# Other recorded distances in stage 1 of a hybrid decoder step: small products, the sample's chunk and the bonus sums

## The chip, the cores and the metric

The kernel runs on one core of a Trainium2 chip. The metric is the device time in microseconds (us) of one execution. Each profile is of one execution, and its rows are of that execution alone. Engines are named as the profile does: PE is TensorE, PEld its weight loads, DVE VectorE, ACT ScalarE, POOL GpSimd and SP SyncE, which issues most DMAs.

## The reference

The reference computes one layer of a decoder for two groups of requests: one prompt of 1024 tokens, and 8 samples of 8 tokens each, which are laid side by side as 1088 columns. Features lie on partitions.

```
h  = adaLN(RMSNorm(x), c)
P  = h @ w_in                       # RWKV columns | pooling columns | gate columns
A  = RWKV-7(P)                      # token shift, decay, delta-rule state per head, group norm, bonus, gate
B  = pooling over windows 2/4/8/16, minus the token, a linear map per group, a scale
x += gate * ((sigmoid(gA) * (A @ w_br_rwkv) + sigmoid(gB) * (B @ w_br_pool)) @ w_out)
h  = adaLN(RMSNorm(x), c)
x += gate * (relu(h @ w_ff1)**2 @ w_ff2)
y  = RMSNorm(x)
```

The state of RWKV-7 follows, per head of 64 values, `S = S*w + (S @ -kk) (kk*a) + v k` and `y = S r`. The bonus is `sum(r*k*r_k) * v` over a head.

## The kernel before, in words

**Stage 1** (`phase1`) computes P, the RWKV and pooling branches and `B @ w_br_pool`; **stage 2** (`phase2`) the rest. The large products are *streamed*: a weight of 128 x 512 is loaded, ACT copies it to `whi` in a 32-bit format that TensorE takes in one pass, and `wlo` = weight - `whi` is made by POOL for odd weights and by DVE for even ones (`weights`). Each column block of 364 or 362 is multiplied three times (hi x hi, hi x lo, lo x hi), so a weight of 512 columns is 36 streamed products (`mm<-hx,whi` and `mm<-hx,wlo` in the rows). At most two weights are held at a time.

Between the streamed products stand the small ones of the heads. The 8 heads go as 4 *pairs* f = 0 to 3, each through these steps:

- `front(f)`: decay and gate logits (`sw` products, tanh), the cumulative decay on DVE, the norm of kk (`bones` products, a square root on ACT, reciprocals on DVE at line 302), the operands `bk` (lines 561 on DVE and 562 on POOL), `q` (568) and the bonus sums (three products with `bones`, then a multiply into `bv` at 577).
- `sample(f - 1)`: the chunk of the samples of the pair before, which has its own state.
- `scores(f)`: three `unit`s (8 chunks of 64 tokens, the samples' chunk, 8 more chunks): products of keys, `ab`/`ak` masks, transposes.
- `inverse`, `level`, `affine`: the inverse of a triangular matrix per chunk, by DVE and then by small products (L726, L737), and what follows from it.
- `chain(f)`: the 16 steps of the state; each is a product with the state S, then a DVE operation that makes the next S (line 828).
- `post(f)`: group norm (`bones` products, reciprocals, lines 926 to 935), bonus and gate.

Beside them `pools` does the pooling groups (`px` and `plw` products, z at lines 457 to 468).

**The order.** Each step is a generator that yields a distance; `Pace` keeps a clock of its own, which every product moves on by an estimate from its shape (a streamed one by n/2.4 + 14 ns). A step whose distance has passed is taken first, and else the next three streamed products are recorded. So the distances alone set where a small product stands in TensorE's order, which is kept as recorded:

```
self.pace.t += n / 2.4 + 14 if rhs.dtype == F32R else max(n / 0.6 * min(mode) / 128, 30) + 3
```

The other engines' queues are ordered by a scheduler, from the recording. Small products write the PSUM tiles `w`, of which there are two, or `wc`, also two; a third waits until the first is read. Five `wt` rows hold the vectors of a pair.

Of the kernel before, what the change touches and what calls it, by code (L numbers as in the profile page):

```python
# [18 lines left out]
P = 128  # L19
# [98 lines left out]
class K:  # L118
    def __init__(self, tc, io):
        self.tc, self.nc, self.io = tc, tc.nc, io  # L120
        self.n = 0
        self.nw = 0
        self.pace = Pace()
        self.mode = None
        self.done = set()

# [27 lines left out]

    def weights(self, src, eng=None):

        nc = self.nc
        n = self.nw
        self.nw += 1
        raw = self.wp.tile([P, 512], F32, tag="wraw", bufs=WB[0], name=self.nm("wraw"))  # L160
        nc.sync.dma_start(raw, src)
        hi = self.wp.tile([P, 512], F32R, tag="whi", bufs=WB[1], name=self.nm("whi"))
        lo = self.wp.tile([P, 512], F32R, tag="wlo", bufs=WB[1], name=self.nm("wlo"))
        nc.scalar.activation(hi, raw, AF.Copy)  # L164
        (eng or (nc.gpsimd if n % 2 else nc.vector)).tensor_tensor(lo, raw, hi.bitcast(F32), op=ALU.subtract)  # L165
        return [(hi[:, q * 128:(q + 1) * 128], lo[:, q * 128:(q + 1) * 128]) for q in range(4)]
# [313 lines left out]
    def pools(self):  # L480

        nc = self.nc
        self.pl = {}
        for g in range(4):
            plw = self.pxp.tile([P, P], F32, tag="plw", bufs=1, name=self.nm("plw"))
            nc.sync.dma_start(plw, self.io["pool_w"][:, g * 128:(g + 1) * 128])
            yield lambda: ("pool", g) in self.done
            yield 5000 + 1300 * g
            z, zs, hi, lo = self.pl[g]
            for c0, n in CH:  # L490
                m = min(n, NPR - c0)
                ps = self.ps("w")
                self.mm(ps[:, :m], plw, z[:, c0:c0 + m], start=True, stop=True)
                if m < n:
                    self.mm(ps[:, m:n], plw, zs, start=True, stop=True)
                sc = self.par("pool_scale", g)
                nc.scalar.activation(hi[:, c0:c0 + n], ps[:, :n], AF.Copy, scale=sc)
                nc.vector.scalar_tensor_tensor(lo[:, c0:c0 + n], ps[:, :n], sc, hi[:, c0:c0 + n].bitcast(F32), op0=ALU.mult, op1=ALU.subtract)
                yield 600
            nc.sync.dma_start(self.d_op[0][g], hi.bitcast(F32))  # L500
            nc.sync.dma_start(self.d_op[1][g], lo.bitcast(F32))
            self.done.add(("op", g))


    def front(self, f):
# [9 lines left out]
        t1, tha = self.wt(), self.wt()  # L515
        yield 9000 if f == 0 else 4500
        for c0, n in CH:
            ps = self.ps("w")
            self.mm(ps[:, :n], w2a2[0:64, :], wa[0:64, c0:c0 + n], start=True, stop=True)
            nc.scalar.activation(t1[:, c0:c0 + n], ps[:, :n], AF.Tanh, bias=self.hp[:, f:f + 1], scale=0.5)  # L520
            ps = self.ps("w")
            self.mm(ps[:, :n], w2a2[64:128, :], wa[64:128, c0:c0 + n], start=True, stop=True)
            nc.scalar.activation(tha[:, c0:c0 + n], ps[:, :n], AF.Tanh, bias=self.hp[:, 4 + f:5 + f], scale=0.5)
            yield 0
        nc.gpsimd.tensor_scalar(t1, t1, 1.0, None, op0=ALU.add)
# [21 lines left out]
        nc.scalar.activation(sq, kk, AF.Square)  # L547
        yield 9000
        for c0, n in CH:
            ps = self.ps("w")  # L550
            self.mm(ps[:, :n], self.kc("bones"), sq[:, c0:c0 + n], start=True, stop=True)
            self.rinv(ps, n, sq[:, c0:c0 + n], 1.0, 1)
            yield 0
        nc.vector.tensor_tensor(kk, kk, sq, op=ALU.mult)
# [10 lines left out]
        nc.sync.dma_start(r, self.d_x[f])  # L565

        q = self.wt()
# [3 lines left out]
        nc.sync.dma_start(v, self.d_x[8 + f])  # L571
        bv = self.wt()
        yield 12000
        for c0, n in CH:
            ps = self.ps("w")
            self.mm(ps[:, :n], self.kc("bones"), q[:, c0:c0 + n], start=True, stop=True)
            nc.vector.tensor_tensor(bv[:, c0:c0 + n], ps[:, :n], v[:, c0:c0 + n], op=ALU.mult)
            yield 0
        nc.sync.dma_start(self.d_bv[f], bv)
        self.cur = dict(bk=bk, end=end, v=v, kk=kk, r=r, ev=ev, es=es, z=self.z, qs={})  # L580

    def scores(self, f, d):

        d["ad"], d["ao"] = self.iv(), self.sm.tile([P, 16, 32], F32, tag="ao", bufs=1, name=self.nm("ao"))
        self.nc.gpsimd.memset(d["ad"][:, NC:32, :], 0.0)
        yield from self.unit(f, d, 0)
        yield from self.unit(f, d, 2)
        yield from self.unit(f, d, 1)

    def unit(self, f, d, u):  # L590
# [17 lines left out]
        else:  # L608
            nc.vector.scalar_tensor_tensor(cut8(ra[:, 0, 1, :]), cut8(kk[:, NPR:NT]), -1.0, es[:, :, 0:8], op0=ALU.mult, op1=ALU.mult)
            nc.gpsimd.tensor_tensor(cut8(ra[:, 0, 0, :]), cut8(r[:, NPR:NT]), es[:, :, 1:9], op=ALU.mult)  # L610
            strict, incl = self.kc("strict8"), self.kc("incl8")
        yield 2500 if prompt else 1200
        for a in range(0, C, 4):
# [8 lines left out]
            for h, (hs, ps) in enumerate(zip(HB, pss)):  # L622
# [4 lines left out]
                for b in range(2):  # L627
# [6 lines left out]
                    else:  # L634
                        nc.vector.tensor_tensor(ad[rq, 16, :], src[:, 0, :], strict[rq, 32 * b:32 * b + 32], op=ALU.mult)
            yield 2500
        bh = bk[:, cs, :, :].rearrange("p c s j -> p c (s j)")
# [39 lines left out]
    def inverse(self, d):  # L677
# [33 lines left out]
        d["zd"], d["xd"], d["n16"] = zd, xd, cut32(n16)  # L711
        yield 2500

    def level(self, d):
# [11 lines left out]
        nc.vector.tensor_tensor(nd, cut32(ps), self.kc("i32").unsqueeze(1).to_broadcast([P, 16, 32]), op=ALU.add)  # L726
        yield 1500
        ps, px = self.ps("w"), self.ps("w")
# [9 lines left out]
        for os in HB:  # L738
            for b in (1, 0):
                rq = slice(os.start + 32 * b, os.start + 32 * b + 32)  # L740
                nc.scalar.activation(z[rq, :16, 32 * b:32 * b + 32], cut32(ps)[rq], AF.Copy)
        yield 1500
        ps = self.ps("w")
# [6 lines left out]
        for os in HB:  # L750
            hi = slice(os.start + 32, os.start + 64)
            nc.scalar.activation(pt[hi], cut32(ps)[hi], AF.Copy)
        yield 1500
        ps = self.ps("w")
# [5 lines left out]
        for os in HB:  # L760
            lo = slice(os.start, os.start + 32)
            nc.scalar.activation(z[lo, :16, 32:64], cut32(ps)[lo], AF.Copy)
        yield 1200

# [39 lines left out]
    def chain(self, f, d):  # L804
# [4 lines left out]
        for u in range(2):  # L809
# [9 lines left out]
            for i in range(8):  # L819
# [11 lines left out]
                S = S1  # L831
                yield LS
            us = slice(u * 512, (u + 1) * 512)
# [11 lines left out]
    def sample(self, f, d):  # L845
# [7 lines left out]
        qm = self.kc("qm")  # L853
        um = iv()
        yield 3000
        px = self.ps("w")
        for h, hs in enumerate(HB):
            os = HB[1 - h]
            if h:
                yield 1500  # L860
            ps = self.ps("w")
            self.mm(ps[os, :], ra[hs, 0, 1, :], s0[hs, :], start=True, stop=True, tile_position=(hs.start, os.start))
            nc.vector.tensor_tensor(qv(um[os]), qv(ps[os, :]), qm[os].unsqueeze(2).to_broadcast([64, 8, 64]), op=ALU.mult)
            self.mm(px[os, 0:64], ak[hs, 0, :], uv[hs, 0, h, :], start=True, stop=True, tile_position=(hs.start, os.start))
        x = sm.tile([P, 64], F32, tag="xs", bufs=1, name=self.nm("x"))
        nc.vector.tensor_reduce(x, um.rearrange("p (q v) -> p v q", v=64), axis=AX.X, op=ALU.add)
        nc.vector.tensor_tensor(x, x, px[:, 0:64], op=ALU.add)
        yield 2500
        for os in HB:
            self.mm(px[os, 64:128], z[os, 16, :], x[os, :], start=True, stop=True)  # L870
        for h, os in enumerate((HB[1], HB[0])):
            nc.scalar.activation(uv[os, 0, h, :], px[os, 64:128], AF.Copy)
        yield 1200
        py = self.ps("w")
# [6 lines left out]
        else:  # L881
            y = sm.tile([P, 64], F32, tag="ys", bufs=1, name=self.nm("y"))
            nc.scalar.activation(y, py[:, :64], AF.Copy)
            nc.sync.dma_start(self.d_y[f][:, NPR:NT], y)
        pn = self.ps("w")
        for h, hs in enumerate(HB):
# [3 lines left out]
            yield 1200  # L890
            self.mm(pn[hs, :], ab[:, 0, h, 64:128], um, start=True, stop=True)
        nc.gpsimd.tensor_tensor(qv(s0), qv(s0), end[:, 16:24].unsqueeze(2).to_broadcast([P, 8, 64]), op=ALU.mult)
# [3 lines left out]
    def post(self, f):  # L896
# [25 lines left out]
        def piece(c0, n):  # L922
# [4 lines left out]
            nc.scalar.activation(sq[:, s], y[:, s], AF.Square)  # L927
            yield 3000
            ps = self.ps("w")
# [39 lines left out]
    def heads(self):  # L969

        for f in range(4):
            yield from self.front(f)
            d = self.cur
            if f > 0:
                yield from self.sample(f - 1, self.ds[f - 1])
            yield from self.scores(f, d)
# [149 lines left out]
    def or_rows(self):  # L1126

        yield lambda: "op" in self.done
        for j in range(3):
            for i in range(2):  # L1130
                t = self.orr[i][j] = self.row(self.hx, "hx", 16, F32R)
# [245 lines left out]
NC = 17  # L1377
LS = 900
WB = (2, 2)
# [72 lines left out]
```

## Time and profile before

| | us |
|---|---|
| median of 3 runs | 1920.29 |
| lowest and highest | 1919.14, 1922.01 |
| the profiled execution | 1926.83 |
| its span, from the first to the last instruction | 1925.1 |
| PE busy in the span | 1765.1 (92%) |
| DVE, ACT, POOL busy | 884.6, 564.1, 374.4 |
| mean granted TensorE clock | 0.946 |

In the page's slices a digit is a tenth of a slice of 48 us. The streamed products begin at 52 us, and stage 2 follows on the reload of rows near 922 to 940 us. In a row of groups the shape of one operation is followed by its count, the busy time, the mean ns of one, and the idle time of the engine just before it with what ended that. In a row of the timeline the brackets hold the idle time ahead of it and what ended that.

### The profile page before, as it was taken

The numbers are of one execution on the slowest core, as the hardware profiler recorded it, in microseconds if no ns is written. First come the engines' busy times: TensorE is split into PE (matmuls) and PEld (weight loads), VectorE is DVE, ScalarE is ACT, GpSimd is POOL, SyncE is SP. The second block draws the span as 40 slices with busy tenths as digits, with TensorE's granted clock in tenths as the row PEclk, the third lists the DMA queues.
The fourth block names the chain that finished last, engine by engine and source line by source line (L and its number), as shares of the span: only waits on it lengthen the run. The fifth ranks groups of instructions, "written<-read, shape, count | busy, mean of one in ns | idle before, by whom it ended". The sixth has DMA issues, their size and how long they took to land. (4 is left out here: it accounts for less than half of the span.)

```text
span 1925.1 us, 32541 instructions
## 1 busy us (share of the span) xinstructions
PE 1765.1 (92%) x13721; PEld 1621.9 (84%) x13721; DVE 884.6 (46%) x1484; ACT 564.1 (29%) x1085; POOL 374.4 (19%) x406
## 2 busy tenths in 40 slices
PE   3889897988799889899899889999999999999997
PEld 1779776876587669789788879999999999999997
DVE  5476445665456455533342664242424242424335
ACT  4424241443134414431122443131313131312132
POOL 1551114101210130001231441111111111111110
PEclk8889788989899899899899989999999999999998
DMA  8232313121322141226772211111111111111112
GB/s 303 73 109 90 108 48 121 56 99 58 124 79 72 55 144 52 71 90 226 265 274 99 77 61 52 48 45 44 45 45 44 44 45 44 44 44 45 44 50 93
DMA packets 76450, 169.97 MB, mean 88 GB/s; under 512 B 15152, under 2 KB 21808, under 8 KB 76304
## 3 DMA queue, kind: packets, MB, share of 16 engines
q1 hardware_dynamic: 70688, 151.68, 22.8%
q10 hardware_dynamic: 5472, 15.70, 2.4%
q8 instruction: 108, 1.77, 0.4%
q0 software_dynamic: 144, 0.51, 0.1%
q14 instruction: 38, 0.31, 0.1%
HBM read 133.47 MB, written 34.39 MB: 87 GB/s over the span
## 5 line engine op out<-in xcount | busy, mean ns | idle before, releaser
L146 PE MATMUL mm<-hx,whi 128*128 128x362 f32 (+1 forms) x2560 | 686.0, 350 | 6.9 <-DMA hx<-d_orl 3.5
L146 PEld LDWEIGHTS mm<-hx,whi 128*128 128x128 f32 x2560 | 461.4, 196 | 47.4 <-issue 21.2
L146 PE MATMUL mm<-hx,wlo 128*128 128x362 f32 (+1 forms) x1280 | 429.6, 336 | 5.2 <-DVE wlo L165 5.0
L165 POOL TENSOR_TENSOR wlo<-wraw,whi 128x512 fp32r<-128x512 f32 x120 | 166.3, 1386 | 1070.9 <-ACT whi L164 1047.2
L146 PE MATMUL mm<-ma,whi 128*128 128x364 f32 (+1 forms) x1280 | 317.6, 329 | 0.0
L164 ACT ACTIVATE whi<-wraw 128x512 fp32r<-128x512 f32 x240 | 151.2, 631 | 559.8 <-PE w L146 395.0
L146 PEld LDWEIGHTS mm<-hx,wlo 128*128 128x128 f32 x1280 | 251.7, 197 | 6.1 <-DVE wlo L165 5.6
L146 PEld LDWEIGHTS mm<-ma,whi 128*128 128x128 f32 x1280 | 225.9, 188 | 5.1 <-issue 4.3
L146 PE MATMUL mm<-ma,wlo 128*128 128x364 f32 (+1 forms) x640 | 210.1, 328 | 0.0
L1330 DVE SCALAR_TENSOR_TENSOR hx<-mm,aq,hx 128x364 f32<-128x364 f32 (+4 forms) x136 | 75.0, 588 | 215.1 <-PE mm L146 214.9
L146 PE MATMUL w<-mb,whi 128*128 128x362 f32 x640 | 164.3, 338 | 6.0 <-DVE mb L1225 2.1
L165 DVE TENSOR_TENSOR wlo<-wraw,whi 128x512 fp32r<-128x512 f32 x120 | 93.6, 780 | 154.0 <-ACT whi L164 153.9
L146 PEld LDWEIGHTS w<-mb,whi 128*128 128x128 f32 x640 | 117.5, 196 | 8.3 <-DVE mb L1225 2.6
L146 PEld LDWEIGHTS mm<-ma,wlo 128*128 128x128 f32 x640 | 120.5, 188 | 0.0
L1243 DVE TENSOR_TENSOR ft<-ft 128x362 f32<-128x362 f32 (+1 forms) x96 | 51.7, 562 | 137.1 <-ACT ft L1242 136.8
L146 PE MATMUL w<-mb,wlo 128*128 128x362 f32 x320 | 107.9, 337 | 7.1 <-DVE wlo L165 5.8
L146 PE MATMUL w<-hx,whi 128*128 128x362 f32 x416 | 104.1, 332 | 0.0
L146 PEld LDWEIGHTS w<-hx,whi 128*128 128x128 f32 x416 | 74.0, 192 | 0.9 <-issue 0.9
L1335 POOL TENSOR_TENSOR hx<-hx,rs 128x64 f32<-128x64 f32 x72 | 36.7, 510 | 187.1 <-DVE rs L1333 187.0
L146 PEld LDWEIGHTS w<-mb,wlo 128*128 128x128 f32 x320 | 62.8, 196 | 8.6 <-DVE wlo L165 7.0
L146 PE MATMUL w<-wt,kct 128*128 128x362 f32 (+1 forms) x96 | 46.0, 586 | 26.1 <-DVE wt L568 10.6
L1242 ACT ACTIVATE ft<-mm 128x364 f32<-128x364 f32 x64 | 29.3, 474 | 134.5 <-PE mm L146 134.4
(295 smaller groups left out, 2374.3 us busy)
## 6 DMA issues: line engine op xcount, KB each, us to landing
wraw<-in_w_ff SPq DMA_DIRECT2D x132, 256.0 KB, 2.6
wraw<-in_w_in SPq DMA_DIRECT2D x68, 256.0 KB, 2.8
t<-in_w_ada_mlp SPq DMA_DIRECT2D x24, 512.0 KB, 5.4
wt<-d_x SPq DMA_DIRECT2D x20, 544.0 KB, 3.9
d_th<-px SPq DMA_DIRECT2D x16, 544.0 KB, 3.3
aw<-in_w_ada_mix SPq DMA_DIRECT2D x16, 512.0 KB, 10.0
wraw<-in_w_out SPq DMA_DIRECT2D x32, 256.0 KB, 2.6
d_x<-d SPq DMA_DIRECT2D x14, 512.0 KB, 2.6
```

What stands on the lines that cost most here:

```text
L146: return self.nc.tensor.matmul(out, lhsT, rhs, **kw)
L164: nc.scalar.activation(hi, raw, AF.Copy)
L165: (eng or (nc.gpsimd if n % 2 else nc.vector)).tensor_tensor(lo, raw, hi.bitcast(F32), op=ALU.subtract)
L1242: nc.scalar.activation(t[:, :n], ps[:, :n], AF.Relu)
L1243: nc.vector.tensor_tensor(t[:, :n], t[:, :n], t[:, :n], op=ALU.mult)
L1330: nc.vector.scalar_tensor_tensor(x[:, c0:c0 + m], ps[:, :m], gt[:, 0:1], x[:, c0:c0 + m], op0=ALU.mult, op1=ALU.add)
L1335: nc.gpsimd.tensor_tensor(x[:, NPR:NT], x[:, NPR:NT], t, op=ALU.add)
```

## The change

Nearly all of it is numbers: the distances that steps of stage 1 yield. Four things are more than that. `weights` makes `wlo` on POOL for the first 68 weights, which are all the halves of `w_in`. The bonus sums leave `front` and become `bonus`, between unit 0 and unit 2 of `scores`. `sample(f - 1)` runs beside `front(f)`, not behind it; it takes its first sums into a tile of their own that ACT copies, adds on POOL, and makes both masked operands before it multiplies. And `or_rows` asks for each row by name.

```diff
+        self.solo = 68
...
-        (eng or (nc.gpsimd if n % 2 else nc.vector)).tensor_tensor(lo, raw, hi.bitcast(F32), op=ALU.subtract)
+        (nc.gpsimd if n % 2 or n < self.solo else nc.vector).tensor_tensor(lo, raw, hi.bitcast(F32), op=ALU.subtract)
...  pools
-            yield 5000 + 1300 * g
+            yield 6000 + 1300 * g
...
-                yield 600
+                yield 1500
...  front: first sums, norm of kk
-        yield 9000 if f == 0 else 4500
+        yield 13000 if f == 0 else 5500
...
-            yield 0
+            yield 1300
...
-        yield 9000
+        yield 10500
...
-            yield 0
+            yield 1000
...  front: bonus
-        bv = self.wt()
-        yield 12000
-        for c0, n in CH:
...
-        self.cur = dict(bk=bk, end=end, v=v, kk=kk, r=r, ev=ev, es=es, z=self.z, qs={})
+        self.cur = dict(q=q, bk=bk, end=end, v=v, kk=kk, r=r, ev=ev, es=es, z=self.z, qs={})
...  scores
         yield from self.unit(f, d, 0)
+        yield from self.bonus(f, d)
         yield from self.unit(f, d, 2)
         yield from self.unit(f, d, 1)
+
+    def bonus(self, f, d):
+        nc, q, v, bv = self.nc, d["q"], d["v"], self.wt()
+        for c0, n in CH:
+            ps = self.ps("w")
+            self.mm(ps[:, :n], self.kc("bones"), q[:, c0:c0 + n], start=True, stop=True)
+            nc.vector.tensor_tensor(bv[:, c0:c0 + n], ps[:, :n], v[:, c0:c0 + n], op=ALU.mult)
+            yield 1000
+        nc.sync.dma_start(self.d_bv[f], bv)
...  unit
-        yield 2500 if prompt else 1200
+        yield 6500 if u == 0 else 3000 if u == 1 else 2000
...
-            yield 2500
+            yield 2800
...  inverse, level
-        yield 2500
+        yield 4500
...
-        yield 1500
+        yield 3000
...
-        yield 1500
+        yield 4000
...
-        yield 1500
+        yield 3000
...
-        yield 1200
+        yield 2500
...  chain
-                yield LS
+                yield LS[f]
...  sample
-        nc.vector.tensor_tensor(x, x, px[:, 0:64], op=ALU.add)
+        nc.gpsimd.tensor_tensor(x, x, x2, op=ALU.add)
+        yield 6000
...  post
-            yield 3000
+            yield 4500
...  heads
-            yield from self.front(f)
+            if f > 0:
+                yield from self.both(self.front(f), self.sample(f - 1, self.ds[f - 1]))
+            else:
+                yield from self.front(f)
...
-LS = 900
+LS = (2300, 2300, 2300, 1500)
```

What this does to the order is shown at three places. The first is PE at the bonus sums of pair 3, where `w<-wt,kct` is a bonus sum and `wt` is q. Before:

```order
L146 MATMUL mm_6182<-hx_159,whi_6171 128x362
L146 MATMUL mm_6182<-hx_160,whi_6171 128x362
L146 MATMUL mm_6182<-hx_159,wlo_6172 128x362
L146 MATMUL w_6271<-wt_6161,kct 128x364
L146 MATMUL w_6274<-wt_6161,kct 128x362
L146 MATMUL w_6277<-wt_6161,kct 128x362
L146 MATMUL mm_6180<-hx_161,whi_6171 128x364
L146 MATMUL mm_6180<-hx_162,whi_6171 128x364
```

Now:

```order
L147 MATMUL w_6688<-uv_6440,ak_6439 64x64 x16
L147 MATMUL mm_6571<-hx_157,whi_6562 128x364
L147 MATMUL mm_6571<-hx_158,whi_6562 128x364
L147 MATMUL mm_6571<-hx_157,wlo_6563 128x364
L147 MATMUL w_6711<-wt_6431,kct 128x364
L147 MATMUL mm_6572<-hx_157,whi_6562 128x362
L147 MATMUL mm_6572<-hx_158,whi_6562 128x362
L147 MATMUL mm_6572<-hx_157,wlo_6563 128x362
L147 MATMUL mm_6573<-hx_157,whi_6562 128x362
L147 MATMUL mm_6573<-hx_158,whi_6562 128x362
```

The three sums stood in a row ahead of unit 0; now the last product of unit 0 (`w<-uv,ak`) stands ahead of them, and 9 streamed products part each from the next.

The second is DVE at the pooled z of group 1 (`px`, lines 467 and 468 before, 468 and 469 now). Before, it stands in the front of pair 2:

```order
L558 TENSOR_TENSOR wt_4217<-wt_4217,wt_4339 128x1088
L559 SCALAR_TENSOR_TENSOR wt_4136<-wt_4136,wt_4218 128x1088
L465 TENSOR_TENSOR zf_4379<-zf_4379,px_3984 128x3
L561 SCALAR_TENSOR_TENSOR bk_4216<-wt_4136,wt_4207 64x17x64 x2
L467 SCALAR_TENSOR_TENSOR px_3984<-px_4372,px_3984 128x1024
L165 TENSOR_TENSOR wlo_4448<-wraw_4445,whi_4447 128x512
L568 SCALAR_TENSOR_TENSOR wt_4349<-wt_4347,part,wt_4217 128x1088
L468 COPY px_3984<-zf_4379 128x3
```

Now:

```order
L782 COPY uv_2786<-w_4014 64x8x64
L465 TENSOR_TENSOR zf_4072<-px_4065,kct 128x3
L471 SCALAR_TENSOR_TENSOR ds_4073<-psm_4069,psm_3662 128x64
L466 TENSOR_TENSOR zf_4072<-zf_4072,px_3661 128x3
L468 SCALAR_TENSOR_TENSOR px_3661<-px_4065,px_3661 128x1024
L469 COPY px_3661<-zf_4072 128x3
L798 TENSOR_TENSOR ra_2787<-ra_2787,w_4098 128x4x64
L798 TENSOR_TENSOR ra_2787<-ra_2787,w_4099 128x4x64
L827 COPY S_4169<-wc_4135 128x64
```

It moved to `affine` and the first step of the chain of pair 1, ahead of pair 2's front.

The third is POOL at the front of pair 0. Before:

```order
L165 TENSOR_TENSOR wlo_900<-wraw_897,whi_899 128x512
L395 COPY ns<-px_785 128x1
L396 COPY ns<-px_785 128x8
L562 TENSOR_TENSOR bk_705<-wt_706,wt_696 64x17x64 x2
L606 TENSOR_TENSOR ra_1050<-wt_821,e_695 128x8x64
L610 TENSOR_TENSOR ra_1281<-wt_821,e_695 128x64
L606 TENSOR_TENSOR ra_1360<-wt_821,e_695 128x8x64
```

Now:

```order
L166 TENSOR_TENSOR wlo_877<-wraw_874,whi_876 128x512
L396 COPY ns<-px_765 128x1
L397 COPY ns<-px_765 128x8
L166 TENSOR_TENSOR wlo_973<-wraw_970,whi_972 128x512
L383 MEMSET px_1051 128x1
L384 COPY px_1051<-sst 128x8
L563 TENSOR_TENSOR bk_787<-wt_788,wt_778 64x17x64 x2
L609 TENSOR_TENSOR ra_954<-wt_942,e_777 128x8x64
```

Every weight's `wlo` now passes through this queue, with bk and ra standing in it as before.

Elsewhere on PE, between two steps of a chain stand 15 streamed products where 6 stood (9 for pair 3), between the second and the third group of a level 24 where 9 stood, and from the last product of pair 3's norm to the end of stage 1 there are 84 where 297 were. Stage 1 has 2736 streamed products in both.

More of the change, by code (lines that the diff above doesn't have):

```diff
@@ L153, in tr, with weights @@
         self.nc.tensor.transpose(out, in_, ident)
-    def weights(self, src, eng=None):
+    def weights(self, src):
         nc = self.nc
@@ L571, in front, with scores @@
         nc.sync.dma_start(v, self.d_x[8 + f])
-        bv = self.wt()
-        yield 12000
+        self.cur = dict(q=q, bk=bk, end=end, v=v, kk=kk, r=r, ev=ev, es=es, z=self.z, qs={})
+    def scores(self, f, d):
+        d["ad"], d["ao"] = self.iv(), self.sm.tile([P, 16, 32], F32, tag="ao", bufs=1, name=self.nm("ao"))
+        self.nc.gpsimd.memset(d["ad"][:, NC:32, :], 0.0)
+        yield from self.unit(f, d, 0)
+        yield from self.bonus(f, d)
+        yield from self.unit(f, d, 2)
+        yield from self.unit(f, d, 1)
+    def bonus(self, f, d):
+        nc, q, v, bv = self.nc, d["q"], d["v"], self.wt()
         for c0, n in CH:
@@ L577, in front @@
             nc.vector.tensor_tensor(bv[:, c0:c0 + n], ps[:, :n], v[:, c0:c0 + n], op=ALU.mult)
-            yield 0
+            yield 1000
         nc.sync.dma_start(self.d_bv[f], bv)
-        self.cur = dict(bk=bk, end=end, v=v, kk=kk, r=r, ev=ev, es=es, z=self.z, qs={})
[L582 to L588, printed above, removed]
     def unit(self, f, d, u):
@@ L854, in sample @@
         um = iv()
+        x, x2 = (sm.tile([P, 64], F32, tag="xs", bufs=2, name=self.nm("x")) for _ in range(2))
         yield 3000
@@ L858, in sample @@
             os = HB[1 - h]
+            self.mm(px[os, 0:64], ak[hs, 0, :], uv[hs, 0, h, :], start=True, stop=True, tile_position=(hs.start, os.start))
+        nc.scalar.activation(x2, px[:, 0:64], AF.Copy)
+        for h, hs in enumerate(HB):
+            os = HB[1 - h]
             if h:
-                yield 1500
+                yield 2500
             ps = self.ps("w")
@@ L863, in sample @@
             nc.vector.tensor_tensor(qv(um[os]), qv(ps[os, :]), qm[os].unsqueeze(2).to_broadcast([64, 8, 64]), op=ALU.mult)
-            self.mm(px[os, 0:64], ak[hs, 0, :], uv[hs, 0, h, :], start=True, stop=True, tile_position=(hs.start, os.start))
-        x = sm.tile([P, 64], F32, tag="xs", bufs=1, name=self.nm("x"))
         nc.vector.tensor_reduce(x, um.rearrange("p (q v) -> p v q", v=64), axis=AX.X, op=ALU.add)
-        nc.vector.tensor_tensor(x, x, px[:, 0:64], op=ALU.add)
-        yield 2500
[L869 to L873, printed above, removed]
+        nc.gpsimd.tensor_tensor(x, x, x2, op=ALU.add)
+        yield 6000
+        px = self.ps("w")
+        for os in HB:
+            self.mm(px[os, 0:64], z[os, 16, :], x[os, :], start=True, stop=True)
+        for h, os in enumerate((HB[1], HB[0])):
+            nc.scalar.activation(uv[os, 0, h, :], px[os, 0:64], AF.Copy)
+        yield 2500
         py = self.ps("w")
@@ L884, in sample @@
             nc.sync.dma_start(self.d_y[f][:, NPR:NT], y)
-        pn = self.ps("w")
-        for h, hs in enumerate(HB):
+        ums = []
+        for h in range(2):
             um = iv()
@@ L889, in sample @@
                                     qm.unsqueeze(2).to_broadcast([P, 8, 64]), op=ALU.mult)
-            yield 1200
-            self.mm(pn[hs, :], ab[:, 0, h, 64:128], um, start=True, stop=True)
+            ums.append(um)
+        yield 4500
+        pn = self.ps("w")
+        for h, hs in enumerate(HB):
+            self.mm(pn[hs, :], ab[:, 0, h, 64:128], ums[h], start=True, stop=True)
         nc.gpsimd.tensor_tensor(qv(s0), qv(s0), end[:, 16:24].unsqueeze(2).to_broadcast([P, 8, 64]), op=ALU.mult)
@@ L927, in piece @@
             nc.scalar.activation(sq[:, s], y[:, s], AF.Square)
-            yield 3000
+            yield 4500
             ps = self.ps("w")
@@ L971, in heads @@
         for f in range(4):
-            yield from self.front(f)
+            if f > 0:
+                yield from self.both(self.front(f), self.sample(f - 1, self.ds[f - 1]))
+            else:
+                yield from self.front(f)
             d = self.cur
-            if f > 0:
-                yield from self.sample(f - 1, self.ds[f - 1])
             yield from self.scores(f, d)
@@ L1129, in or_rows @@
         for j in range(3):
+            yield lambda: ("or", j) in self.done
             for i in range(2):
```

## The prediction

> **What bounds the kernel now.** I read first the slices of the page, then a table of stretches, then the waits of TensorE in the stretch that stands out.
>
> ```profile
> span 1925.1 us, 32541 instructions
> PEclk8889788989899899899899989999999999999998
> 57.00:838.00 781.00, 693.70 (x7338) 591.19 (x7338) 423.04 (x664) 270.93 (x560) 160.43 (x177) 0.91 0.25 87
> 922.00:940.00 18.00, 13.18 (x49) 11.17 (x53) 3.13 (x6) 0.63 (x1) 1.66 (x2) 0.62 0.70 271
> 1160.00:1925.00 765.00, 750.98 (x4537) 747.30 (x4535) 283.94 (x541) 169.73 (x334) 109.50 (x126) 0.99 0.15 48
> ```
>
> A row of stretches holds the length, then busy time and count of PE, PEld, DVE, ACT and POOL, then the granted clock. TensorE is the bound throughout, but only from 1160 us on does it run undisturbed: 751.0 of 765 us busy at clock 0.99. In 57 to 838 us, the part of stage 1 in which small products of the heads stand between the streamed ones, it idles 781.00 - 693.70 = 87.3 us, and the mean clock is 0.91. No other engine comes near: DVE has 423.0 of 781 us. The gap at 922 us is the reload of rows from DRAM between the stages, which the change leaves where it is.
>
> The idle time has names (who waited, for whom, us in total, times, longest):
>
> ```profile
> PE w L146 <- DVE px L468: 13.8, 2, 12.4
> PE wc L146 <- DVE S L828: 11.5, 9, 2.9
> PE w L146 <- DVE wt L568: 10.6, 2, 7.0
> PE w L146 <- DVE hv L737: 6.1, 5, 2.5
> PE w L146 <- ACT iv L631: 5.1, 6, 1.4
> PE mm L146 <- DVE wlo L165: 5.0, 2, 4.0
> PE w L146 <- DVE wt L577: 4.9, 2, 4.0
> PE w L146 <- ACT wt L547: 4.4, 4, 1.6
> PE w L146 <- ACT wt L300: 3.9, 8, 0.8
> PE w L146 <- issue: 3.7, 1, 3.7
> PE w L146 <- ACT wt L520: 3.5, 7, 0.9
> PE w L146 <- ACT wt L933: 3.4, 1, 3.4
> PE w L146 <- DMA wt<-d_x: 2.5, 1, 2.5
> PE w L146 <- DVE wt L926: 2.3, 1, 2.3
> PE w L146 <- DVE x L867: 2.2, 1, 2.2
> ```
>
> TensorE takes its instructions in the order written. So a small product whose operand is late holds every streamed product behind it. Nearly all of the list is of that kind: not too little work, but a product that stands too early.
>
> **A stall costs more than its idle time.** After a late step of a chain (second row: a stretch of windows at the clock's own edges; last row: the sum over four such stretches, 213.78:234.26, 299.12:309.36, 483.44:497.09 and this one):
>
> ```profile
> 634.10 0.48 PE L146 MATMUL wc<-S,ra 64*64 64x64 f32 x4 [2.90 <-DVE S L828]
> 633.62:640.45 6.83, 6.35 (x54) 5.23 (x54) 1.84 (x7) 0.77 (x2) 0.00 (x0) 0.50 0.00 0
> sum 51.20, PE 33.97 PEld 26.67 DVE 19.19 ACT 6.70 POOL 13.53; mean PE 8.49 PEld 6.67 DVE 4.80 ACT 1.68 POOL 3.38
> 603.81 0.33 PE L146 MATMUL mm<-hx,wlo 128*128 128x362 f32 x1
> 604.30 0.32 PE L146 MATMUL mm<-hx,wlo 128*128 128x362 f32 x1
> 614.80 0.50 PE L146 MATMUL mm<-hx,wlo 128*128 128x362 f32 x1
> 615.70 0.50 PE L146 MATMUL mm<-hx,wlo 128*128 128x362 f32 x1
> ```
>
> The granted clock after the stall of 2.90 us is 0.50. Three streamed products take 604.30 - 603.81 = 0.49 us before such a stretch (0.163 us each) and 615.70 - 614.80 = 0.90 us in one. A mean of 0.91 over 781 us means 2 x 0.09 x 781 = 140 us at half clock. TensorE was busy in 33.97 of 51.20 us (66%) of the four stretches and in 93% of the last, so 93 to 130 of the 140 us were work at half speed, which lost 46 to 65 us. I take 55. The stretch thus loses about 87 + 55 = 142 us, and each microsecond of stall costs 1 + 55/87 = 1.63 us.
>
> The Trainium skill ("TensorE: Matmul & The Clock Gate", table of why this matters) says to allow no idle gap over about 3 us, since one idle window of about 3.4 us halves the clock. Here 2.90 us was enough, so the row decides. By the rule the whole 55 us would hang on the gaps over 3.4 us (12.4, 7.0, 4.0, 4.0, 3.6, 3.7), of which the sum below removes all but the 3.7; that is 90% of 55 where the sum takes 35, an estimate of 15 us more gain.
>
> **The change part by part.** The products, their shapes and the streamed work stay, but for the sample's sum of um, which gets a PSUM tile of its own and an extra copy on ACT; what changes is where the small products stand, and which engine makes wlo. Distances are counted in the built order; one streamed product is 0.163 us.
>
> *Bonus sums behind unit 0.* They were three products in a row right after the front, waiting for q (line 568), then for the multiply that frees their PSUM tile (577). Now unit 0 lies between q and the first sum, and 9 streamed products between the sums (1.5 us, against a multiply of some 0.5 us). Of 10.6 + 4.9 us I remove 15.
>
> *Pool sums of group 1.* The wait of 12.4 us is DVE's queue:
>
> ```profile
> 479.56 7.02 POOL L562 TENSOR_TENSOR bk<-wt,wt 64x1088 f32<-64x1088 f32 x2 [9.32 <-DVE wt L558]
> 477.99 0.15 DVE L464 TENSOR_TENSOR zf<-px,kct 128x3 f32<-128x3 f32 x1
> 480.60 2.44 DVE L465 TENSOR_TENSOR zf<-zf,px 128x3 f32<-128x3 f32 x1
> 482.97 4.76 DVE L561 SCALAR_TENSOR_TENSOR bk<-wt,wt 64x1088 f32<-64x1088 f32 x2
> 492.61 0.16 DVE L468 COPY px<-zf 128x3 f32<-128x3 f32 x1
> ```
>
> The pooled z stood among the vector work of pair 2's front (bk, 4.76 us, and more). In the new order it is done before that front, among pair 1's chain. The rest of that row (1.4 us, group 2) stays. Remove 12.4.
>
> *Chain of states.* Between two steps stand 15 streamed products, not 6: 9 x 0.163 = 1.5 us more for pairs 0 to 2 (pair 3 has 9, and showed no wait). Nine waits have a mean of 1.3 us and a longest of 2.9, so those up to 1.5 us go and the three over 2 us keep about 1 each. Remove 8.5 of 11.5.
>
> *Inverse's level.* From the second to the third product group 24 streamed products, not 9: 2.5 us. Waits on line 737 were at most 2.5 us, and the one for line 933 was 3.4. Remove 8.2 of 9.5.
>
> *Front's first sums* (520, the load of d_x, 547, 300; together 14.3 us). The first products of pair 0 stand 24 streamed products (3.9 us) later, against a wait of 2.5; the next ones 1.5 us later against at most 1.6; and 9 products now part the chunks. Line 300 is partly in the group norm, where chunks stay close. Remove 11.
>
> *Sample and norm.* From the sample's mask to its next product there are 6 us of recorded distance, not 2.5, though shared with the front: the 2.2 us go. Norm's squares 1.5 us later: 1.5 of 2.3. Units 0.5 us later against waits of mean 0.9: 2.5 of 5.1.
>
> *wlo on POOL.* In stage 1 all 68 subtractions run on POOL. Groups of 57 to 838 us:
>
> ```profile
> L165 POOL TENSOR_TENSOR wlo<-wraw,whi 128x512 fp32r<-128x512 f32 x32 | 50.9, 1590 | 410.5 <-ACT whi L164 394.3 <-PE w L146 16.1
> L562 POOL TENSOR_TENSOR bk<-wt,wt 64x1088 f32<-64x1088 f32 x8 | 26.5, 3312 | 16.3 <-DVE wt L558 16.0
> L165 DVE TENSOR_TENSOR wlo<-wraw,whi 128x512 fp32r<-128x512 f32 x32 | 30.9, 967 | 26.5 <-ACT whi L164 26.5
> ```
>
> DVE is rid of 30.9 us and POOL gains 32 x 1.59 = 51 us (160 to 211 of 781). A wlo must be ready within one weight's 36 products (5.9 us) and the small work between. Only behind the two bk of a front (2 x 3.3 + 1.6 = 8.2 us) is that close: 0 to 4 us at four places, 0 to 16 us; I take 4, since the POOL half of the wlo passed the same bk with hardly a wait. The sample's x + x2, which moves to POOL too, waits there for DVE's reduce with a wlo behind it; that is in the 4. The 5.0 us of waits for DVE's wlo go.
>
> The Trainium skill ("SBUF — State Buffer", who interferes with whom) says that a DVE operation with two SBUF inputs is locked out for the whole of a GpSimd operation that reads SBUF. The rows agree: 2.44 us for a form that took 0.15, beside bk on POOL. By that rule alone 51 us of new POOL work could lock DVE for 20 us more than the 30.9 us it saves; if TensorE idled for all of that, 33 us of the gain would go, an estimate of 1863.
>
> *New crowding.* Front and sample now run beside each other on two "w" tiles of PSUM; group 3's sums fall into a level. By the nearest waits (line 520: 3.5 us in 7) a crowded place costs 0.5 us: some 13 places, 7 us; bounds 0 and 14.
>
> *End of the stage.* The last product of the last norm now stands 84 streamed products (13.7 us) before stage 2; before, 297. Behind it is vector work of pair 3's last chunk, on this row's chain:
>
> ```profile
> 870.91 2.43 DVE L302 RECIPROCAL wt<-wt 128x182 f32<-128x182 f32 x2 [0.62 <-ACT wt L300]
> 875.49 0.54 DVE L935 TENSOR_TENSOR wt<-wt,wt 128x362 f32<-128x362 f32 x1
> ```
>
> 875.49 + 0.54 - 870.91 = 5.1 us, so the streamed products cover it: nothing. Without that cover it would cost up to 5 us. The new condition in or_rows is met by then, since pair 2's norm ends some 400 streamed products earlier, and the same six loads go to SP's queue.
>
> **The sum.** Removed: 15 + 12.4 + 8.5 + 8.2 + 11 + 2.2 + 1.5 + 2.5 + 5.0 = 66.3 us of idle time. New: 4 + 7 = 11. Net 55, times 1.63 = 90 us. The profiled execution took 1926.83 us (1.7 more than its span) and would take 1837; the median of the runs, 1920.29, lies 6.5 lower, which gives **1830 us**. Bounds: with half of the terms that rest on a queue (all but the first two and wlo: 33.9, so 17 less) and 30 new, 19 net or 31 us, 1889; with 76 removed and nothing new, 124 us, 1796.
>
> **Rivals.**
> (a) *The stalls move.* DVE is a queue: with 90 us less, its 392 us stand in 691, 57% against 54%, sample's and front's work meet in it, and a product placed later meets another late operand. For it: 5 of the 15 rows are DVE queues, and the 12.4 us shows how long one gets. Against it: DVE idles 46% of the stretch. Net 25 us of idle time, 41 us of time: 1879.
> (b) *POOL's wlo becomes the bound; slower.* Every weight passes through one in-order POOL queue, behind bk, ra and additions that themselves wait for DVE and ACT; DVE loses time to POOL as in the row of 2.44 us. It decides when the moved wlo are late by more than 55/34 = 1.6 us each, on the mean; at 1.9 us each (65 us, times 1.63) the time is 1936. Against it: the POOL half waits 410.5 us for whi, not the reverse.
> (c) *It doesn't do what it says.* The distance is counted in the recording's own clock, and DVE and ACT follow a scheduler's order; if that fills the new distance with other work ahead of the operand, the same operands are late: 1920.
>
> **Chances and range.** Forecast (1796 to 1862) 0.70, (a) 0.19, (c) 0.04, (b) 0.07. The range of 8 in 10 reaches into (a): 1797 to 1882. Three runs spread by 2.9 us, so 0.2% (3.8 us) is about what can be told from no change: faster 0.89 (forecast and (a)), the same 0.04, slower 0.07.
>
> **What would show it.** Right: from 57 us to the gap of the reload the stretch is some 90 us shorter, with idle time near 32 us and a mean clock of 0.96 or more; no row for q or for px of 10 us; S under 4 us; DVE's wlo gone from the waits. Wrong: waits of streamed products on POOL's wlo over 10 us (b), or a list as long with other names (a); a wait at the head of stage 2 for the last norm would show that the end isn't covered.

## The result, and the profile after

The changed kernel takes **1866.11 us** (median of 4 runs, 1863.12 to 1868.98), the kernel before 1921.15 (4 runs, 1919.14 to 1924.67): ratio 0.971, interval 0.969 to 0.973, so 55 us faster. The forecast was 1830. The profiled execution took 1863.12 us, the shortest of its four, and that of before 1926.83, 5.7 above its median. So the two profiles differ by 63.7 us, and those 63.7 us, not the 55, are what can be taken apart.

The first view is the table of stretches, from 57 us to the same streamed product in the reload of rows (length, PE busy with its count, granted clock, DMA share, GB/s). Before:

```profile
57.00:941.00 884.00, 789.77 (x7896) 0.91 0.28 98
```

After:

```profile
57.00:878.00 821.00, 744.82 (x7904) 0.95 0.31 106
```

The stretch is 63 us shorter, so all of the gain lies here. But of the idle time only 94.2 - 76.2 = 18 us went, where the prediction had 55. The other 45 us are less busy time for the same products (789.77 - 744.82).

The waits of TensorE in that stretch, after (who waited, for whom, us in total, times, longest):

```profile
PE w L147 <- POOL ra L609: 39.0, 4, 11.0
PE w L147 <- DVE hv L729: 5.4, 3, 2.1
PE w L147 <- issue: 4.4, 2, 2.7
...
PE w L147 <- DVE wt L936: 3.8, 1, 3.8
PE w L147 <- ACT iv L634: 2.8, 4, 1.4
...
PE w L147 <- ACT wt L521: 2.7, 3, 1.4
...
PE w L147 <- ACT wt L548: 2.3, 1, 2.3
...
PE wc L147 <- DVE S L831: 0.7, 2, 0.5
...
```

The rows of 13.8 (px), 11.5 (S), 10.6 (q) and 5.0 us (wlo) of before are gone or small. In their place stands one row that before did not have at all: half of the idle time, in four pieces of 9.1 to 11.0 us. Its first piece, on PE, POOL and DVE (start, us, instruction, and in brackets the idle time ahead of it and what ended that):

```profile
134.54 0.87 PE L147 MATMUL w<-ra,bk 64*128 64x128 f32 x4 [10.97 <-POOL ra L609]
...
125.37 6.93 POOL L563 TENSOR_TENSOR bk<-wt,wt 64x1088 f32<-64x1088 f32 x2 [4.70 <-DVE wt L559]
132.38 2.10 POOL L609 TENSOR_TENSOR ra<-wt,e 128x512 f32<-128x512 f32 x1
...
119.33 1.22 DVE L303 RECIPROCAL wt<-wt 128x180 f32<-128x180 f32 x1
...
126.53 6.93 DVE L562 SCALAR_TENSOR_TENSOR bk<-wt,wt 64x1088 f32<-64x1088 f32 x2
```

This is the first product of unit 0 of pair 0. From the last reciprocal of the front (its end, 120.55) to POOL's ra (134.48) runs a chain of 13.9 us, and unit 0 now stands 6500 ns of recorded distance behind the front. In the kernel before, the bonus sums' 12000, unit 0's own 2500 and, for pairs 1 to 3, the whole chunk of the samples stood between them.

### The profile page after: what moved, and what is told of

It reads as the page before. It is cut to its first block, busy times and chain, and to the rows that moved or that the text cites. A ratio compares the mean times of both kernels' runs of the same rounds, so it can differ in the third digit from the quotient of the medians.

```text
span 1861.3 us, 32532 instructions
## 1 busy us (share of the span) xinstructions
PE 1720.2 (92%) x13721; PEld 1597.2 (86%) x13721; DVE 867.1 (47%) x1446; ACT 557.6 (30%) x1085; POOL 421.9 (23%) x444
## 5 line engine op out<-in xcount | busy, mean ns | idle before, releaser
L147 PEld LDWEIGHTS mm<-hx,whi 128*128 128x128 f32 x2560 | 456.8, 193 | 54.4 <-issue 23.1
L166 POOL TENSOR_TENSOR wlo<-wraw,whi 128x512 fp32r<-128x512 f32 x154 | 206.6, 1342 | 1047.0 <-ACT whi L165 1031.7
L147 PE MATMUL mm<-hx,wlo 128*128 128x362 f32 (+1 forms) x1280 | 425.0, 332 | 0.0
L147 PEld LDWEIGHTS mm<-hx,wlo 128*128 128x128 f32 x1280 | 247.9, 194 | 0.0
L166 DVE TENSOR_TENSOR wlo<-wraw,whi 128x512 fp32r<-128x512 f32 x86 | 61.2, 712 | 126.9 <-ACT whi L165 126.9
L303 DVE RECIPROCAL wt<-wt 128x182 f32<-128x182 f32 (+1 forms) x48 | 57.8, 1251 | 29.1 <-ACT wt L301 29.1
```

What stands on the lines that cost most here:

```text
L147: return self.nc.tensor.matmul(out, lhsT, rhs, **kw)
L166: (nc.gpsimd if n % 2 or n < self.solo else nc.vector).tensor_tensor(lo, raw, hi.bitcast(F32), op=ALU.subtract)
L303: nc.vector.reciprocal(out[:, a:min(a + 182, n)], out[:, a:min(a + 182, n)])
```

## The experiments

All idle and busy times are PE's in the profiled execution, from 57 us to the same streamed product in the reload (within 1 us). A ratio is against the kernel before, run on the same chip. The runs were made on several chips, on which the median of the kernel before lay between 1916.82 and 1921.15 us; so a difference of a few us between two rows is to be read from the ratios, and where their intervals overlap it isn't shown.

| run | us, median | ratio, interval | idle | busy |
|---|---|---|---|---|
| before | 1921.15 | | 94.2 | 789.8 |
| the change | 1866.11 | 0.971 (0.969 to 0.973) | 76.2 | 744.8 |
| e1_cover | 1848.56 | 0.964 (0.960 to 0.968) | 51.3 | 748.7 |
| e2_front | 1864.10 | 0.971 (0.968 to 0.974) | 66.8 | 752.2 |
| e3_bonus | 1943.02 | 1.013 (1.009 to 1.017) | 101.6 | 797.4 |
| e4_ls | 1878.45 | 0.979 (0.975 to 0.984) | 91.6 | 738.4 |
| e5_solo | 1862.90 | 0.971 (0.966 to 0.976) | 76.5 | 743.5 |
| e7_level | 1883.16 | 0.981 (0.976 to 0.986) | 85.3 | 752.7 |
| e8_early | 1846.16 | 0.963 (0.959 to 0.967) | 56.7 | 744.3 |
| e9_both | 1841.84 | 0.961 (0.956 to 0.966) | 52.3 | 744.7 |
| e10_room | 1837.43 | 0.957 (0.953 to 0.961) | 51.3 | 741.7 |
| e11_ls | 1855.55 | 0.966 (0.963 to 0.970) | 60.3 | 751.7 |

My theory after the result was that the row for ra is a lost cover: whatever product stands first behind a front waits for DVE's and POOL's backlog, and the change moved the two things that had stood there. The rivals were that POOL's new load makes ra late, and that the stalls only change their name.

### The distance ahead of unit 0 (e1_cover)

```diff
-        yield 6500 if u == 0 else 3000 if u == 1 else 2000
+        yield 17500 if u == 0 else 3000 if u == 1 else 2000
```

> The changed kernel with 17500 in place of 6500 ahead of the first product of unit 0; nothing else. In the changed kernel that product waits for POOL's ra (line 609) 11.0, 9.1, 9.3 and 9.6 us, 39.0 us at four places, and these stalls cost about 44 us with the half clock behind them. Theory (the cover is missing: bonus sums and sample stood between bk, ra and unit 0, and both went): the ra row falls under 4 us. But the streamed products run out sooner: by the recorded distances 24 us of small work at the end of stage 1 stand bare, where the changed kernel has all covered. So 1866 - 44 + 24 = 1846 us. Rival (the stalls only move: PE has no more work that can run, or DVE's and POOL's queue is what is late): another row of 25 us or more appears inside the stage, and with the bare end it is 1875 or more.

Measured: 1848.56 us. Its waits:

```profile
PE wc L147 <- DVE S L831: 11.7, 9, 3.5
...
PE w L147 <- POOL ra L609: 5.2, 1, 5.2
...
PE w L147 <- ACT wt L937: 3.6, 3, 1.2
```

The row for ra fell from 39.0 to 5.2 us, as the theory said, and the last norm (L937) stands bare at the end. What neither had expected is the first row: the waits for S are back, as much as before the change (11.7 against 11.5 us), with 2300 between the steps. The longest of them, on PE and DVE:

```profile
311.89 0.48 PE L147 MATMUL wc<-S,ra 64*64 64x64 f32 x4 [3.51 <-DVE S L831]
...
304.61 6.92 DVE L562 SCALAR_TENSOR_TENSOR bk<-wt,wt 64x1088 f32<-64x1088 f32 x2
311.55 0.28 DVE L831 SCALAR_TENSOR_TENSOR S<-S,end,wc 128x64 f32<-128x64 f32 x1
```

An operation of 0.28 us stands in DVE's queue behind 6.92 us of bk. In the changed kernel TensorE stands still for ra while DVE makes bk (above: 123.57 to 134.54 against 126.53 to 133.46; at pair 1, where a chain runs beside it, 297.40 to 306.50 against 298.56 to 305.41). No step of a chain can ask for S in that time, so it seems that such a wait is hidden there; `e11_ls` below bears that out only in part.

### The bonus alone, on the kernel before (e3_bonus)

```diff
-        yield 12000
-        for c0, n in CH: ...            # bonus sums, in front
...  scores
         yield from self.unit(f, d, 0)
+        yield from self.bonus(f, d)
...  unit
-        yield 2500 if prompt else 1200
+        yield 6500 if u == 0 else 2500 if prompt else 1200
```

> The kernel before with the bonus sums behind unit 0 and no other part of the change (6500 ahead of unit 0, 1000 between the sums, as in the change). Theory (missing cover): for pairs 1 to 3 the sample still stands between the front and unit 0, so nothing new is late there; only pair 0, which has no sample, waits for ra, once, about 10 us. The waits on q and on the bonus' multiply (10.6 and 4.9 us) go: 5 us of idle time less, 1912 us. Rival (POOL is late because all wlo pass through it now): wlo is not moved here, so no row for ra, and the full 15 us go: about 1896.

Measured: 1943.02 us, *slower* than before by 1.3%, and the interval stays above 1; neither had that. The waits:

```profile
PE w L146 <- DVE x L870: 15.0, 2, 8.6
...
PE w L146 <- POOL ra L609: 8.1, 1, 8.1
```

The ra of pair 0 waits 8.1 us, as the theory said, with wlo where it was. For pairs 1 to 3 I had taken the sample as a cover. But the sample now stands first behind the front, and its own x (2.2 us before, 15.0 now, at pairs 1 and 2) waits in the same queue:

```profile
291.19 3.49 DVE L561 SCALAR_TENSOR_TENSOR bk<-wt,wt 64x1088 f32<-64x1088 f32 x1
294.71 1.04 DVE L869 TENSOR_REDUCE x<-hv 128x64 f32<-128x512 f32 x1
295.66 2.33 DVE L568 SCALAR_TENSOR_TENSOR wt<-wt,part,wt 128x1088 f32<-128x1088 f32 x1
297.92 0.21 DVE L870 TENSOR_TENSOR x<-x,w 128x64 f32<-128x64 f32 x1
```

x's reduce stands behind bk, and between it and its 0.21 us addition stands q. So the wait belongs to the place, not to the operand.

### The bonus in front again, in the changed kernel (e2_front)

```diff
+        yield 12000
+        yield from self.bonus(f, dict(q=q, v=v))
         self.cur = dict(q=q, bk=bk, ...)
...  scores
-        yield from self.bonus(f, d)
```

> The changed kernel with the bonus sums in front of unit 0 again, 12000 behind the front as before; nothing else undone. Theory (the wait belongs to the place, the first product behind a front, and not to its operand): no row for ra, but one for q (line 568, which stands behind bk on DVE), about 5 us at each of four places, 20 us in all; and 30 us of small work at the end of stage 1 stand bare: 1866 - 44 + 20 + 8 + 30 = 1880. Rival (ra alone is late): the row for q stays under 5 us, 1852.

Measured: 1864.10 us. Its first and largest row:

```profile
PE w L147 <- DVE wt L568: 26.7, 4, 9.1
```

There is no row for ra, and q has taken its place, at the same four fronts. That settles the place. The time came out 16 us under what I had expected, and I had counted 30 us of bare work at the end: the row for the last norm (line 938) shows 6.6 us in 3 waits. Within the changed kernel the edit "bonus behind unit 0" is thus worth nothing that can be measured: 1864.10 against 1866.11, both at a ratio of 0.971.

### wlo on both engines again (e5_solo)

```diff
-        self.solo = 68
+        self.solo = 0
```

> The changed kernel with wlo made by DVE and POOL in turn, as before; nothing else. Theory (missing cover): no wlo stands on POOL between bk and ra, so the row of 39.0 us for ra stays within 3 us, and DVE's wlo comes back into the waits with up to 5 us; time 1866 to 1874. Rival (POOL's new load makes ra late): the row for ra falls by half or more, 1845 or less.

Measured: 1862.90 us, within the interval of the change. The row for ra stays:

```profile
PE w L147 <- POOL ra L609: 41.1, 4, 13.0
```

The rival that POOL's load makes ra late falls. It also says that this edit is worth nothing that can be measured, for good or ill. Nor does a row for DVE's wlo come back, though DVE makes half of the wlo again.

### Earlier operands (e8_early, e9_both)

```diff
+        m = ...; k = k * m              # ahead of the norm's products
+        for h, hs in enumerate(HB):
+            nc.gpsimd.tensor_tensor(bk[hs, :, h, :], cut(k[hs]), cut(ei[hs]), op=ALU.mult)
         sq = self.wt()
         nc.scalar.activation(sq, kk, AF.Square)
         yield 10500
...                                      # the same lines go from behind the norm
```

> The changed kernel with the operands of unit 0 made earlier and no distance changed: m, k*m and POOL's half of bk (which need nothing of the norm of kk) are recorded ahead of the norm's products, not behind them. From the end of the last reciprocal to unit 0's first product DVE then has 1.3 + 1.3 us and its own bk, 4.8 us when POOL is not beside it (6.9 us with POOL), in place of 13.9 us. Theory (missing cover, so the length of the chain to bk and ra counts): the row for ra or bk at unit 0 falls from 39.0 to about 16 us, and the time to about 1840. Rival (what unit 0 waits for is set by the queues, not by this chain): the row stays over 30 us, 1860 or more.

Measured: 1846.16 us, 20 less than the change (ratio 0.963 against 0.971). The row for ra, with no distance changed:

```profile
PE w L147 <- POOL ra L610: 14.0, 4, 4.3
```

So the length of the chain counts. Part of it was the two engines side by side. The groups of bk (count: ns least, median, most), in the changed kernel and then in e8_early:

```profile
L563 POOL TENSOR_TENSOR bk<-wt,wt x8: 3408/3430/3455, 125.4 to 663.1; 64x1088 f32<-64x1088 f32 x8
L562 DVE SCALAR_TENSOR_TENSOR bk<-wt,wt x8: 3359/3448/3457, 126.5 to 664.2; 64x1088 f32<-64x1088 f32 x8
```

```profile
L551 POOL TENSOR_TENSOR bk<-wt,wt x8: 2483/2506/2524, 107.4 to 631.8; 64x1088 f32<-64x1088 f32 x8
L564 DVE SCALAR_TENSOR_TENSOR bk<-wt,wt x8: 1273/1284/1290, 125.2 to 645.4; 64x1088 f32<-64x1088 f32 x8
```

Apart, the four operations of a front take 2 x 2.51 + 2 x 1.28 = 7.6 us; side by side they took from 125.37 to 133.46, 8.1 us. There was no gain in doing them at once. The Trainium skill ("SBUF — State Buffer", Who interferes with whom) says that such a pair excludes each other for whole instructions; the sum of 7.6 against the 8.1 us agrees.

`e9_both` goes further: (1 + tha) * ei ahead of the norm too, and r loaded early.

```diff
+        nc.vector.scalar_tensor_tensor(tha, tha, 1.0, ei, op0=ALU.add, op1=ALU.mult)
         sq = self.wt()
...
+        yield X(f)
+        r = self.wt()                    # ahead of the norm's products
```

> As e8_early, and three things more on the same chain, with no distance changed: (1 + tha) * ei is made ahead of the norm's products too, so that behind the last reciprocal DVE has only kk (1.3 us) and its own bk (2.6 us as measured in e8_early); and since ei is then read for the last time early, r is loaded into its row ahead of those products, so that POOL's ra no longer waits for that load (in e8_early the load landed 3.9 us before ra could start). Theory (what unit 0 waits for is the length of this chain): the row for ra or bk at unit 0 falls from 14.0 us to under 3, and the four stretches of half clock of 6.8 us there go; 14 of idle time and about 2.5 us for each of four stalls: 1846 - 24 = 1822, at most 1830. Rival (a floor is reached, the waits only get another name): other rows grow by as much, 1840 or more.

Measured: 1841.84 us, 4 less than e8_early, where I had expected 24; as the two intervals overlap, even the 4 aren't shown. The rival was nearer:

```profile
PE w L147 <- DVE ra L612: 6.6, 3, 2.8
PE w L147 <- ACT wt L554: 6.6, 3, 3.8
```

The stalls at unit 0 shrank from 14.0 to 10.7 us (these 6.6 and 4.1 for line 608 at pair 0), now for DVE's half of ra. The norm's sq (line 554), which had become late in e8_early already (4.9 us in 2 waits), grew to 6.6.

### The chain's distance (e4_ls, e11_ls)

```diff
-LS = (2300, 2300, 2300, 1500)
+LS = (900, 900, 900, 900)
```

> The changed kernel with 900 between the steps of a chain, as before (6 streamed products in place of 15 or 9); nothing else. Theory (the prediction's term: the distance removed the waits for S): the row for S, 0.7 us in the changed kernel, returns to 8 us or more, and with the price of a stall the time is 14 to 18 us longer, about 1881. Rival (the waits for S went because DVE was rid of wlo and of the front's backlog, not by the distance): S stays under 3 us and the time within 4 us of 1866.

Measured: 1878.45 us. The time is what my term for the chain gave, and its reason is wrong: S is as good as absent, and ra has grown.

```profile
PE w L147 <- POOL ra L609: 49.4, 4, 14.2
...
PE wc L147 <- DVE S L831: 0.2, 1, 0.2
```

Whether S was absent because the stalls at ra hid it, `e11_ls` asks, with the long distance of e1_cover beside the same edit.

> As e1_cover, with 900 between the steps of a chain. In e1_cover the waits for S came back (11.7 us), with the long distance; in e4_ls (900 between the steps, but 6500 ahead of unit 0) there were none. Theory (a step waits for S where it stands among or behind the front's norm of kk, in DVE's queue; with 900 all steps stand ahead of the norm's products): S under 3 us; the end of stage 1 stands 2.7 us barer: 1849 - 11 + 3 = 1841. Rival (the distance between two steps decides, and e4_ls had no waits only because the stalls at ra hid them): S 12 us or more, 1855 or more.

Measured: 1855.55 us, the rival's time, but S fell to less than half:

```profile
PE w L147 <- POOL ra L609: 11.7, 3, 5.3
...
PE wc L147 <- DVE S L831: 4.4, 9, 1.8
```

The shorter distance did not lengthen the waits for S, so the distance is not what decides; that all steps standing ahead of the front's norm frees them is only half borne out, since nine waits, of half a microsecond on the mean, are left. What ended those nine I didn't follow. Nor did the time gain by it: ra grew by 6.5 us, nearly what S lost.

### The level's distances (e7_level)

```diff
-        yield 4500 / 3000 / 4000 / 3000 / 2500    # inverse, then level
+        yield 2500 / 1500 / 1500 / 1500 / 1200
```

> The changed kernel with the distances of inverse and level as before (2500, 1500, 1500, 1500, 1200); nothing else. Theory (the prediction's term): the rows for hv, z, iv and the group norm's wt, about 12 us in the changed kernel, grow by 8 us, and the time by about 13 to 16 us: 1880. Rival (these waits depend on what else meets in the two w tiles, not on the distance): the sum of these rows stays within 3 us, and the time within 4 us of 1866.

Measured: 1883.16 us, 17 more, as the term had it. But not where it had it: the rows for hv, iv and the norm's wt (lines 729, 634 and 936), 12 us in the changed kernel, are smaller (1.2 us), and others are longer. The two rows that the term was read from, lines 737 and 933 of the kernel before, are lines 740 and 943 here; they come back, but with 3.5 us only.

```profile
PE w L147 <- POOL ra L609: 45.5, 4, 13.6
...
PE w L147 <- ACT wt L943: 2.4, 2, 2.1
...
PE w L147 <- DVE hv L740: 1.1, 3, 0.4
```

9 us of the 17 are idle time and 8 busy time. Which of the five distances carries it stays open.

### A version that beats both (e10_room)

```diff
-        yield 6500 if u == 0 else 3000 if u == 1 else 2000
+        yield 8500 if u == 0 else 3000 if u == 1 else 2000
...  front, as e9_both, but
+        sq = self.wt()                   # ahead of m; m goes into bk's own tile
```

> As e9_both, with 8500 in place of 6500 ahead of unit 0 (2 us more at each of four places, 8 of the 13.7 us that still cover the last norm), and with sq recorded ahead of m (m goes into bk's own tile, so that sq doesn't wait for m's row). In e9_both unit 0 still waits 4.1, 1.8, 2.0 and 2.8 us for ra, and the norm's first product 3.8 and 2.2 us for sq. Theory (each stall costs its length and about 2.5 us of half clock, however short it is): unit 0's waits fall to 3 us in all, those for sq to 2.5; 12 us of idle time and four to five stalls: 1842 - 22 + 2 for the end = 1822, at most 1830. Rival (as in e1_cover a longer distance lets the waits for S come back): S 8 us or more, 1838 or more.

Measured: 1837.43 us (1831.39 to 1841.25), ratio 0.957; 4 us less than e9_both, though the two intervals overlap. S did not come back (0.7 us), against the rival. The time I had expected, 1822, was not reached either:

```profile
...
PE w L147 <- DVE ra L608: 6.0, 1, 6.0
...
```

Pair 0 still waits 6.0 us, now because DVE makes bk and q ahead of ra, and the rows for iv and issue have grown (2.8 and 3.9 us in e9_both, 5.8 and 8.7 here). Between e8_early and e10_room idle time fell from 56.7 to 51.3 us only: in these runs, removing one wait mostly gave the next its turn.

## Why the prediction was right or wrong

**Right: direction, place, and most of the terms.** The gain lies in stage 1, between 57 us and the reload, and in stalls of small products. With ra left aside, 94.2 - 76.2 + 39.0 = 57 us of idle time went, against a net of 55 in the sum. q and the bonus' multiply (15) are gone; px (12.4) is gone; of the front's first sums 14.3 - 5.5 = 8.8 went (11 were expected); the units gave 5.1 - 2.8 = 2.3 (2.5); the level's two rows are gone (9.5, with 8.2 expected); x and DVE's wlo are gone. Only the norm's squares went the other way (2.3 to 3.8 us, where 1.5 were to go). POOL's wlo has no row, so the 4 us for it were not needed, and rival (b) fell. The end of the stage is covered: the head of stage 2 has no wait for the last norm. Most of this is read from rows alone. The move of px, the distances of the front's first sums and those of the sample were undone by no run, and DVE's wlo went without the edit that was to remove it, since it stays away in e5_solo too.

**Wrong: "Bonus sums behind unit 0 ... Of 10.6 + 4.9 us I remove 15".** This step asked what the moved product no longer waits for, and not what then stands first in its place. I had written that small products wait for late operands, and had quoted bk with 7.02 and 4.76 us; yet unit 0, which needs that bk and POOL's ra behind it, went into the sum with "Units 0.5 us later: 2.5". The distances were there to be added: 6500 now, where 12000, 2500 and a chunk of samples had stood. The profile puts 39.0 us in this place, and e1_cover, e2_front and e8_early show the cause. With them the net is 55 - 39 = 16 us, near the 18 measured. That is what rival (a) names, with a net of 25, at four places and all with one cause. By the prediction's own signs the mechanism was thus in large part (a)'s: the rows named there went, but the stretch is 63 us shorter and not 90, and idle time is 76 us and not 32.

**Wrong in its basis, and right in size by luck: 1.63 us for each us of stall.** By that rate the net of 18 us of idle time would have given 29 us, 11 of them by the clock; 63.7 were measured, 45 of them busy time. All stretches at half clock from 57 us to the reload (the sums of 20 stretches before, and of 13 after):

```profile
sum 153.61, PE 125.74; mean PE 6.29
sum 86.74, PE 56.56; mean PE 4.35
```

If work at half clock loses half of its time, that is 62.9 us before and 28.3 after, so about 35 of the 45 us are clock. It is the size that the sum had, but the sum had tied it to 55 us of idle time, of which 18 went. The other 10 us stood in no term: small products of the same shape and number that are themselves shorter. The front's first sums are such a group, before and after:

```profile
L146 PE MATMUL w<-wt,sw 64*128 64x362 f32 x32 | 13.9, 689 | 3.5 <-ACT wt L520 3.5
L147 PE MATMUL w<-wt,sw 64*128 64x362 f32 x32 | 7.5, 516 | 0.0
```

The sample's last products (`w<-hv,ab`) are another, with 9.5 us before and 4.3 after. A part of both differences is clock again, and why the rest is shorter no run here shows.

The half clock does not follow the length of a stall. The stretches of half clock around the four stalls at ra, in the changed kernel (the sum of four, the first from 126.67 to 140.32 us: length, PE busy):

```profile
sum 44.37, PE 18.25; mean PE 4.56
```

and in e8_early, where they had shrunk from 39.0 to 14.0 us:

```profile
sum 27.32, PE 22.34; mean PE 5.58
```

Work at half clock is 18.25 us behind the long stalls and 22.34 behind the short ones: by the same half it lost 9 and 11 us, so about 2.5 us a stall, for stalls of 2.7 to 11.0 us alike. By this estimate a stall of 10 us costs 1.2 us for each of its own; one of 2 us, where it brings the half clock on, more than 2. The change took stretches of half clock away, though it added four long stalls. So the forecast's 90 us come apart as 37 us of idle time too much and 10 us of shorter products too little: 63, of the 63.7 measured.

**Right in size, wrong in cause: the chain, and in part the level.** "Remove 8.5 of 11.5" for S: 10.8 went. But with the old distance S does not return (e4_ls, 0.2), and with the new one it does (e1_cover, 11.7). The waits go with DVE's backlog of the front, not with the number of products between two steps; that the stalls at ra covered part of them in the changed kernel is likely and not shown. "Remove 8.2 of 9.5" for the level: all 9.5 went, but the old distances bring back only 3.5 of them (e7_level), and yet cost 17 us. The term paid, mostly by other rows than those it was read from. And the new distances made rows grow that the sum didn't have: the waits for line 729, the same operation as line 726 before, went from 1.5 to 5.4 us.

**The range** held the time; the likeliest one's own, up to 1862, missed it by 4 us, for the reason above.

## What to carry to other kernels

On an engine that runs in order, a wait belongs to the first instruction behind a backlog, not to the operand that the profile names: before a product is moved out of a place, work out when the *next* one's operands are ready, by adding up the queue that makes them. Shortening that queue (e8_early, 20 us, no distance changed) was worth about as much as a longer distance (e1_cover, 17.5 us), and a longer distance is paid for at the end, where the work that should cover it runs out (3.6 us for the last norm in e1_cover). And count stalls, not only their sum: a short one that brings the half clock on cost as much clock here as a long one.

## What the runs showed of the hardware

Half clock came in stretches of whole multiples of 3.41 us, and within one trace all their edges lie on one grid of that step. It takes less than such a length of idling to bring one on, though not always. In the changed kernel a gap of 2.14 us was followed by one (the wait on PE's timeline, then the grid's window that holds it and the next):

```profile
747.65 0.77 PE L147 MATMUL w<-wt,kct 128*128 128x362 f32 x1 [2.14 <-DVE hv L729]
744.48:747.89 3.41, 1.25 (x18) 1.00 0.40 131
747.89:751.30 3.41, 3.41 (x11) 0.50 0.00 0
```

In e10_room a gap of 2.52 us was not. It lies across an edge of the grid, so that the window ahead of the edge idles 0.99 us and the next 1.54, where the window above idles 2.16:

```profile
649.78 0.38 PE L147 MATMUL w<-ra,bk 64*128 64x128 f32 x2 [2.52 <-DVE ra L612]
644.83:648.24 3.41, 2.42 (x20) 1.00 0.16 33
648.24:651.66 3.42, 1.88 (x26) 1.00 0.59 206
```

The Trainium skill ("TensorE: Matmul & The Clock Gate", What's actually happening) has a free-running window of that length, which would let the same gap fall either way; these windows agree. Its advice to allow no gap over about 3 us (table of why this matters) is too generous here.

Nor does it take a gap at all. In the changed kernel a window without idle time was followed by half clock; 2.2 us of it are 32 of the sample's products of only 8 columns (the two windows, then that group):

```profile
454.35:457.76 3.41, 3.41 (x41) 1.00 0.70 202
457.76:461.17 3.41, 3.41 (x63) 0.50 0.11 26
L147 PE MATMUL w<-ra,hv 64*64 64x8 f32 x32 | 2.2, 201 | 0.0
```

So not all of the half clock hangs on stalls. That such small products count as idling is a guess that no run here tests.

Besides, DVE's bk took 1.28 us alone and 3.45 beside POOL's, which itself went from 2.51 to 3.43.
